# Experts' loop: transposes, combine, gather and the S5 operators in pieces between weight tiles, and six more weight buffers

## The chip, the cores and the metric

The kernel runs on one core of one Trainium2 chip. The metric is the device time of one execution in microseconds (us). One launch computes the whole model.

## What is computed

All in float32, for 512 tokens of 1024 channels: a first block (a convolution branch and a recurrent branch, then a mixture of experts), and a second block (attention and a gated feed-forward layer, then a state space layer, S5, and again a feed-forward layer). The change lies in the mixture of experts, in which each of 16 experts picks its 64 best tokens:

```python
def expert_choice_moe(h, p):
    cap = EC_CAPACITY * T // N_EXPERTS                      # 2 * 512 / 16 = 64
    affinity = jax.nn.softmax(h @ p['router_w'], axis=-1)
    gates, idx = lax.top_k(jnp.swapaxes(affinity, 1, 2), cap)
    xe = jax.vmap(lambda hb, ib: hb[ib])(h, idx)
    hid = jax.nn.silu(einsum('becd,edf->becf', xe, p['exp_w1'])) * einsum('becd,edf->becf', xe, p['exp_w3'])
    ye = einsum('becf,efd->becd', hid, p['exp_w2']) * gates[..., None]
    return jax.vmap(lambda ib, yb: zeros((T, D)).at[ib.reshape(-1)].add(yb.reshape(-1, D)))(idx, ye)
```

Each expert's w1 and w3 are 1024 x 2048, its w2 is 2048 x 1024: 16 experts have 402.65 MB of weights, which are read once. S5's operators (the taps of a convolution inside chunks of 8 tokens, and the map from a chunk to the state) depend on that layer's parameters alone; the kernel computes them early, beside the experts, and keeps them in DRAM.

## The kernel before

Experts are taken in eight pairs, j = 0 to 7 (`moe`, L1512). A pair reads 48 weight tiles of 128 x 2048 (1 MiB), in order: 16 of w1 and w3 for each of the two experts, then 16 of w2. SP issues each load (`pair_weight`, L1331) as soon as its buffer is free. Pairs 1 to 7 have the stream's six buffers (`open_stream`, L1225); pair 0 has fifteen, nine of them in memory that is given back afterwards (`open_early`).

Inside a pair, for each expert e and each of four groups fb of four w13 tiles: PE multiplies the 64 gathered tokens (XG) with the four tiles, the products for w1 above those for w3 (L1537); ACT copies the result out of PSUM (hs, L1543); PE transposes it in four parts (L1546); ACT takes the tanh (L1549) and DVE makes silu times the other product from it (L1550, L1551), which gives hid. After both experts come the w2 tiles, two at a time (L1580). At the pair's end ACT copies the result (ye, L1604), DVE makes the scaled one-hot matrix Gt (L1607), and eight matmuls (L1613) with one PSUM buffer spread ye over the tokens; after each of them DVE adds it to acc (L1619; in pair 0 it copies, L1617).

The next pair's tokens are gathered after the first expert (`gather`, L1477): PE selects the indices (L1484), DVE compares (oh, L1488), 32 products with the one-hot matrix follow (L1505, each recorded as two), and ACT writes XG (L1509).

`s5_prep` (L1969) begins at the end of pair 0: a set-up on DVE, then eight pieces q. For each, an engine (POOL for q = 1, 4, 6, DVE for the others) makes complex products, big (also called CA) and Winc, by `cmul` (L1957, L1958: pairs of products and their sum); PE transposes Winc in two halves (L2058), ACT copies them (sst, L2060) and stores them (s5i, L2061); the same engine makes a block-diagonal factor bbd (L2064, L2068); PE multiplies big by it (L2072) and ACT and DVE finish a slice of KT (L2075, L2076). big and Winc have a name for each engine (bigv, Wincv, bigg, Wincg) and one buffer for each name. In the source, one step of this stands behind each group of four tiles.

The order of the source isn't the order on the engines: the framework's scheduler orders each engine's instructions, and each engine then works through its own list. The rows of the list are shown below where they matter.

```python
        pool, n = self.early[x % len(self.early)] if self.early else (None, 0)
        w = self.wslot("we") if pool is None else pool.tile([P, 2048], F32, name="we", tag="we", bufs=n)
        self.nc.sync.dma_start(w, src)
```

## Time and profile before

| | us |
|---|---|
| median of 3 runs | 3466.82 |
| lowest and highest | 3463.49, 3468.05 |
| span of the profiled execution | 3452.7 |
| PE busy in it | 3168.8 (92%) |
| DVE busy in it | 1735.9 (50%) |
| ACT busy in it | 963.4 (28%) |
| POOL busy in it | 672.3 (19%) |

The span is that of one execution from its first to its last instruction; the profiled execution's own time isn't given, and the median of the runs lies 14.1 us above the span. The experts' first load is issued at 895.7 us in the span; their pairs begin at 983 (pair 0), 1110.6, 1298.4, 1424.3, 1549.8, 1677, 1804 and 1930 (pair 7), and end at 2056. The rows read are in a section below. In them PE is the matmul, PEld the load of its stationary operand, and an arrow in square brackets names what an engine had waited for.

### The profile page before, as it was taken

What the parts mean: (1) busy time and instruction counts of PE and PEld (TensorE: products, weight loads), DVE (VectorE), ACT (ScalarE), POOL (GpSimd) and SP (SyncE); (2) the same over time, 40 slices, a digit from 0 to 9 for tenths busy, and PEclk for the clock granted to TensorE, in tenths of its full rate; (3) what the DMA queues carried; (4) which work ended last, traced back from release to release, by engine and by line L of the source; (5) the groups of instructions that cost most, each with busy time, mean ns of one, the idle gap of its engine ahead of it and who ended that gap; (6) DMA issues with size and microseconds to landing.
All of it is one profiled execution on the core that took longest, in us unless ns stands there. A gap on an engine that the chain in (4) does not pass through costs nothing.

```text
span 3452.7 us, 41189 instructions
## 1 busy us (share of the span) xinstructions
PE 3168.8 (92%) x15981; PEld 1954.8 (57%) x15981; DVE 1735.9 (50%) x3105; ACT 963.4 (28%) x1799; POOL 672.3 (19%) x703
## 2 busy tenths in 40 slices
PE   8988999999999689999999989799888998999999
PEld 3746566666563333233333227565767877778887
DVE  4656777664451831101101117887477775556464
ACT  3303444443121111111001013227332332234242
POOL 1032234332110520000000003310397002110000
PEclk9989989898899899999999999899999999999999
DMA  5743211112568589999999984320335555522221
GB/s 213 249 163 97 68 47 47 44 35 99 218 240 338 214 341 395 411 410 386 402 406 389 396 339 159 134 87 18 112 117 207 177 200 139 154 87 94 95 98 67
DMA packets 145481, 681.33 MB, mean 197 GB/s; under 512 B 25455, under 2 KB 34839, under 8 KB 77320
## 3 DMA queue, kind: packets, MB, share of 16 engines
q1 hardware_dynamic: 135520, 652.99, 50.0%
q0 software_dynamic: 5392, 17.64, 1.4%
q10 hardware_dynamic: 4376, 8.09, 0.7%
q8 instruction: 126, 2.06, 0.2%
q14 instruction: 67, 0.55, 0.0%
HBM read 654.54 MB, written 24.12 MB: 197 GB/s over the span
## 4 chain that ended last, share of the span: by engine, by line
PE 51%; DMA 8%; POOL 7%; DVE 6%; ACT 2%; issue 2%; SPq 0%; ACTq 0%; POOLq 0%; DVEq 0%
PE mm L1537 12%; DMA we<-in_w_dram 7%; PE mm L284 5%; PE mm L285 5%; PE mm L286 5%; PE ch L1580 3%; POOL cug L1957 3%; PE tr L1505 2%; PE sm L1613 2%; POOL sca L1958 2%; PE sm L286 1%; PE sm L285 1%; PE sm L284 1%; PE tr L1546 1%; PE ch L284 1%
## 5 line engine op out<-in xcount | busy, mean ns | idle before, releaser
L1537 PE MATMUL mm<-we,XG 128*64 128x512 f32 x2048 | 495.3, 608 | 4.8 <-DMA we<-in_w_dram 4.1
L1537 PEld LDWEIGHTS mm<-we,XG 128*64 128x64 f32 x2048 | 139.3, 138 | 292.2 <-issue 269.0
L1580 PE MATMUL ch<-we,hid 128*64 128x512 f32 x1024 | 278.2, 601 | 26.3 <-DMA we<-in_w_dram 26.3
L284 PE MATMUL mm<-hh,wh 128*128 128x512 f32 x704 | 282.7, 402 | 20.7 <-DVE vg L1911 16.4
L285 PE MATMUL mm<-hl,wh 128*128 128x512 f32 x704 | 278.7, 396 | 0.0
L286 PE MATMUL mm<-hh,wl 128*128 128x512 f32 x704 | 272.9, 396 | 0.0
L1550 DVE SCALAR_TENSOR_TENSOR hth<-hth,tr 128x256 f32<-128x256 f32 x64 | 26.9, 420 | 446.2 <-ACT hth L1549 446.1
L1580 PEld LDWEIGHTS ch<-we,hid 128*64 128x64 f32 x1024 | 95.4, 136 | 201.7 <-issue 139.1
L1619 DVE TENSOR_TENSOR acc<-acc,sm 128x512 f32<-128x512 f32 x48 | 33.0, 687 | 292.1 <-PE sm L1613 292.1
L284 PEld LDWEIGHTS mm<-hh,wh 128*128 128x128 f32 x704 | 134.7, 191 | 63.5 <-issue 27.0
L1543 ACT ACTIVATE hs<-mm 128x512 f32<-128x512 f32 x64 | 38.2, 597 | 465.7 <-PE mm L1537 448.8
L1626 POOL TENSOR_TENSOR ess<-ess,mhalf 128x1 f32<-128x1 f32 x4 | 2.6, 650 | 811.3 <-DVE ess L1625 811.2
L346 DVE SCALAR_TENSOR_TENSOR macc<-wa,cvs,macc 128x512 f32<-128x512 f32 (+1 forms) x119 | 152.8, 1300 | 12.9 <-DMA wa<-in_adaw_dram 10.4
L279 DVE TENSOR_TENSOR wl<-wu,wh 128x1024 fp32r<-128x1024 f32 x88 | 115.4, 1312 | 80.5 <-ACT wh L278 80.2
L286 PEld LDWEIGHTS mm<-hh,wl 128*128 128x128 f32 x704 | 134.8, 191 | 29.6
L285 PEld LDWEIGHTS mm<-hl,wh 128*128 128x128 f32 x704 | 135.3, 192 | 26.7 <-POOL hl L455 0.3
L461 POOL TENSOR_TENSOR X<-X,gy 128x512 f32<-128x512 f32 x20 | 28.2, 1434 | 587.6 <-DVE gy L1643 587.6
L278 ACT ACTIVATE wh<-wu 128x1024 fp32r<-128x1024 f32 x88 | 93.2, 1060 | 131.5 <-PE mm L285 98.6
L279 DVE TENSOR_TENSOR wl<-wd,wh 128x1024 fp32r<-128x1024 f32 (+1 forms) x48 | 56.0, 1168 | 95.3 <-ACT wh L278 91.0
L284 PE MATMUL mm<-hTh,wh 128*128 128x512 f32 x208 | 88.3, 425 | 6.1 <-ACT th L795 5.5
L278 ACT ACTIVATE wh<-wd 128x1024 fp32r<-128x1024 f32 (+1 forms) x48 | 47.5, 989 | 164.0 <-PE sm L286 79.6
L286 PE MATMUL mm<-hTh,wl 128*128 128x512 f32 x208 | 88.3, 424 | 3.5 <-DVE wl L279 3.5
(841 smaller groups left out, 6753.9 us busy)
## 6 DMA issues: line engine op xcount, KB each, us to landing
we<-in_w_dram SPq DMA_DIRECT2D x384, 1024.0 KB, 9.5
wu<-in_wupf_dram SPq DMA_DIRECT2D x44, 1024.0 KB, 4.8
wa<-in_adaw_dram SPq DMA_DIRECT2D x24, 1024.0 KB, 5.1
wa<-in_adaw_dram SPq DMA_DIRECT2D x96, 256.0 KB, 4.1
wa<-in_modw_dram SPq DMA_DIRECT2D x16, 1024.0 KB, 5.7
wd<-in_wdn_dram SPq DMA_DIRECT2D x16, 1024.0 KB, 4.8
aw<-in_awin_dram SPq DMA_DIRECT2D x12, 1024.0 KB, 5.0
wi<-in_win_dram SPq DMA_DIRECT2D x46, 256.0 KB, 2.7
```

Source lines behind the costliest of these rows:

```text
L278: self.nc.scalar.activation(h, x, AF.Copy)
L279: (E or self.nc.vector).tensor_tensor(l, x, h.bitcast(F32), op=OP.subtract)
L284: mm(ps, a[0], b[0], start=start, stop=False)
L285: mm(ps, a[0], b[1], start=False, stop=False)
L286: mm(ps, a[1], b[0], start=False, stop=stop)
L346: V.scalar_tensor_tensor(a, w, c, a, op0=OP.mult, op1=OP.add)
L1505: nc.tensor.matmul(ps[:, c * i:c * i + c], self.xn[:, t, o:o + P], oh[:, t], start=(t == 0), stop=(t == TT - 1), skip_group_check=True)
L1537: nc.tensor.matmul(ps[64 * h:64 * h + 64], XG[:, k, CAP * e:CAP * e + CAP], w[:, i, h], start=(k == 0), stop=(k == KD - 1), skip_group_che ...
L1580: nc.tensor.matmul(py[n][64 * h:64 * h + 64], hid[h][:, f], ww[h][:, i, 512 * n:512 * n + 512], start=(f == 0), stop=(f == 15), skip_group ...
L1613: nc.tensor.matmul(pc, G[:, P * t:P * t + P], ye[:, 512 * n:512 * n + 512], start=not last, stop=True, skip_group_check=last)
L1957: E.tensor_tensor(u[k], p[k][1], p[k][0], op=OP.mult)
L1958: E.tensor_tensor(o, u[0], u[1], op=op)
```

## The change

1. The transposes, tanh and gate products of a group of four tiles (`gated`) are issued behind the first tile of the next group.
2. The gather of the next pair is a generator that is stepped behind the first tile of each group of the second expert, so that its selection, and two halves of the channels, come apart.
3. The combine of a pair is a generator too, stepped in the next pair: one matmul and one addition behind each of the second to fourth tiles of a group. Only the last pair does it at once, and its sums of the experts before (`moe_sum`) stand inside the w2 tiles.
4. `s5_prep` makes the vector products of a piece (`vectors`, now with bbd) a step ahead of its matmuls (`products`); even pieces go to DVE, odd ones to POOL; bbd has a buffer for each engine; it is stepped twelve times in a pair, and what is left of it is done when pair 3 begins. s5k is stored from POOL's queue.
5. From pair 3 on, when the memory of `s5_prep` is given back, every second weight tile goes into a pool of six more buffers (`late`).

Comments are removed as well, which is left out here.

```diff
     def pair_weight(self, j, x):
...
-        src = self.I["w13"][2 * j + x // 16, x % 16] if x < 32 else self.I["w2"][j, x - 32]
...
         pool, n = self.early[x % len(self.early)] if self.early else (None, 0)
         w = self.wslot("we") if pool is None else pool.tile([P, 2048], F32, name="we", tag="we", bufs=n)
-        self.nc.sync.dma_start(w, src)
+        self.nc.sync.dma_start(w, self.weight_src(j, x))
...
+    def weight_src(self, j, x):
+        return self.I["w13"][2 * j + x // 16, x % 16] if x < 32 else self.I["w2"][j, x - 32]
...
     def gather(self, j, wk):
...
             for t in range(TT):
                 nc.vector.tensor_scalar(oh[:, t], po[:, :P], self.m("tcol")[:, t:t + 1], None, op0=OP.is_equal)
+            yield
             parts = [(oh, XG)]
...
     def moe(self):
...
+        NJ = NEXP // 2
...
                 g0 = self.gather(0, wk)
                 nxt = next(g0)
-                prep = ()
+                prep, late, acc, MG = (), None, None, None
+                turn = cycle(range(2))
                 def weight(x):
-                    return self.first_w[x] if j == 0 and x < len(self.first_w) else self.pair_weight(j, x)
-                for j in range(NEXP // 2):
+                    if j == 0:
+                        return self.first_w[x] if x < len(self.first_w) else self.pair_weight(j, x)
+                    if late is None or next(turn):
+                        return self.pair_weight(j, x)
+                    w = late.tile([P, 2048], F32, name="we", tag="we", bufs=6)
+                    nc.sync.dma_start(w, self.weight_src(j, x))
+                    return w
+                def gated(hs, hT, fb):
+                    pt = self.psum("tr", 2)
+                    for i in range(4):
+                        nc.tensor.transpose(pt[:, P * i:P * i + P], hs[:, P * i:P * i + P], self.ident)
+                    pv = pt.rearrange("p (i h s) -> p i h s", i=4, h=2)
+                    th = wk.tile([P, 4, CAP], F32, name="hth")
...
+                def combine(j, G, ye):
...
+                        for n in range(2):
+                            pc = self.psum("sm", 1)
+                            nc.tensor.matmul(pc, G[:, P * t:P * t + P], ye[:, 512 * n:512 * n + 512], start=True, stop=True)
+                            s = slice(512 * n, 512 * n + 512)
+                            if j == 0:
+                                nc.vector.tensor_copy(acc[:, t, s], pc)
+                            else:
+                                nc.vector.tensor_tensor(acc[:, t, s], acc[:, t, s], pc, op=OP.add)
+                            yield
+                def run():
+                    nonlocal pend
+                    if pend is not None:
+                        gated(*pend)
...
+                pend, comb, gat = None, iter(()), iter(())
+                for j in range(NJ):
                     XG = nxt
+                    last = j == NJ - 1
+                    if j == 3:
+                        for _ in prep:
+                            pass
+                        s5s.close()
+                        late = self.pool(es, "late", side="right")
                     hid = []
                     for e in range(2):
                         hT = wk.tile([P, 16, CAP], F32, name="hid", bufs=3)
                         hid.append(hT)
+                        if e and not last:
+                            gat = self.gather(j + 1, wk)
                         for fb in range(4):
                             ps = self.psum("mm", 2)
                             for kq in range(4):
                                     for h in range(2):
                                         nc.tensor.matmul(ps[64 * h:64 * h + 64], XG[:, k, CAP * e:CAP * e + CAP], w[:, i, h],
                                                          start=(k == 0), stop=(k == KD - 1), skip_group_check=True)
-                            if j:
-                                for _ in islice(prep, 1):
-                                    pass
+                                if kq == 0:
+                                    run()
+                                    if e:
+                                        nxt = next(gat, None) or nxt
+                                else:
+                                    next(comb, None)
+                                if j and (kq == 0 or kq == 2 and fb % 2):
+                                    next(prep, None)
                             hs = wk.tile([P, 512], F32, name="hs")
                             nc.scalar.activation(hs, ps, AF.Copy)
-                            pt = self.psum("tr", 2)
...
+                            pend = hs, hT, fb
...
-                        if e == 0 and j < NEXP // 2 - 1:
-                            nxt, *_ = self.gather(j + 1, wk)
-                    last = j == NEXP // 2 - 1
...
-                        sums = {}
-                        for i, tag in enumerate(("mm", "mm", "tr", "tr", "sm", "pp")):
-                            sums[i // 2, i % 2] = self.moe_sum(tag, acc, i // 2, i % 2)
                     py = [self.psum("ch", 2) for _ in range(2)]
                     for q in range(8):
                         ww = []
...
-                    if last:
-                        for _ in prep:
-                            pass
+                        if q == 0:
+                            run()
+                            for _ in gat:
+                                pass
+                        if q == 2 and last:
+                            sums = {}
+                            for i, tag in enumerate(("mm", "mm", "tr", "tr", "sm", "pp")):
+                                sums[i // 2, i % 2] = self.moe_sum(tag, acc, i // 2, i % 2)
...
-                            prep = self.s5_prep(self.pool(es, "s5p", side="right"))
+                            prep = self.s5_prep(self.pool(s5s, "s5p", side="right"))
+                            next(prep)
...
                         G = wk.tile([P, T], F32, name="Gt", bufs=1)
                         nc.vector.tensor_scalar(G, self.m("iota"), self.gcol[:, 0, j:j + 1], self.gcol[:, 1, j:j + 1],
                                                 op0=OP.is_equal, op1=OP.mult)
-                    ss = wk.tile([P, TT, 2], F32, name="ess", bufs=1)
-                    for t in range(TT):
...
-                            nc.tensor.matmul(pc, G[:, P * t:P * t + P], ye[:, 512 * n:512 * n + 512], start=not last, stop=True,
-                                             skip_group_check=last)
-                            s = slice(512 * n, 512 * n + 512)
-                            if j == 0:
-                                nc.vector.tensor_copy(acc[:, t, s], pc)
-                            elif not last:
-                                nc.vector.tensor_tensor(acc[:, t, s], acc[:, t, s], pc, op=OP.add)
-                            else:
-                                sums[t, n] = pc
...
+                    if not last:
+                        comb = combine(j, G, ye)
+                ss = wk.tile([P, TT, 2], F32, name="ess", bufs=1)
+                for t in range(TT):
...
...
-        for q in range(KD):
-            E = G if q in (1, 4, 6) else V
-            t = "v" if E is V else "g"
+        def vectors(q):
...
+            E, t = ((V, "v"), (G, "g"))[q % 2]
             s = slice(NQ * q, NQ * q + NQ)
             CA = wk.tile([P, 1152], F32, name="big" + t).rearrange("p (r i c j) -> p r i c j", r=2, i=NQ, c=16)
...
-            yield
             self.cmul(E, wk, *[W[:, r].rearrange("p i c j -> p i j c") for r in range(2)],
...
+            bd = wk.tile([P, 2, NQ, 2, 16], F32, name="bbd" + t)
+            E.memset(bd, 0.0)
+            for g in range(2):
+                rs = slice(64 * g, 64 * g + 64)
+                for r in range(2):
+                    E.tensor_scalar(bd[rs, r, :, g], bb[rs, r, s], 1.0 - 2 * r, None, op0=OP.mult)
+            return CA, W, bd
+        def products(q, CA, W, bd):
             for r in range(2):
                 ps = self.psum("pp", 1)
                 for i in range(NQ):
...
                 st = wk.tile([P, 512], F32, name="sst", bufs=2)
                 nc.scalar.activation(st, ps, AF.Copy)
                 nc.scalar.dma_start(self.s5i[q, :, r], st.rearrange("p (i c) -> p i c", c=P))
-            yield
-            bd = wk.tile([P, 2, NQ, 2, 16], F32, name="bbd")
-            E.memset(bd, 0.0)
-            for g in range(2):
-                rs = slice(64 * g, 64 * g + 64)
-                for r in range(2):
-                    E.tensor_scalar(bd[rs, r, :, g], bb[rs, r, s], 1.0 - 2 * r, None, op0=OP.mult)
+                yield
...
-        nc.sync.dma_start(self.s5k[:, :, 112:].rearrange("q p x -> p q x"), KT.rearrange("p q j c -> p q (j c)"))
+        yield
+        ops = None
+        for q in range(KD + 1):
+            new = vectors(q) if q < KD else None
+            yield
+            if ops is not None:
+                yield from products(q - 1, *ops)
+            ops = new
+        nc.gpsimd.dma_start(self.s5k[:, :, 112:].rearrange("q p x -> p q x"), KT.rearrange("p q j c -> p q (j c)"))
```

Where this puts the instructions is seen in the lists of the engines.

PE in the first group of pair 4 (sm: the combine of pair 3; mm: the product with w1 and w3; tr: the transposes; misc is the identity). Before, from the sixth combine product on:

```order
L1537 MATMUL mm<-we,XG 64x512 x2
L1613 MATMUL sm<-ye,Gt 128x512
L1537 MATMUL mm<-we,XG 64x512 x2
L1613 MATMUL sm<-ye,Gt 128x512
L1537 MATMUL mm<-we,XG 64x512 x4
L1546 MATMUL tr<-misc,hs 128x128 x4
L1537 MATMUL mm<-we,XG 64x512 x3
```

and with the change, from the fourth on:

```order
L1552 MATMUL sm<-ye,Gt 128x512
L1588 MATMUL mm<-we,XG 64x512 x4
L1552 MATMUL sm<-ye,Gt 128x512
L1540 MATMUL tr<-misc,hs 128x128 x4
L1588 MATMUL mm<-we,XG 64x512 x4
L1552 MATMUL sm<-ye,Gt 128x512
L1588 MATMUL mm<-we,XG 64x512 x4
```

Before, all eight combine products stood in the group's four tiles, with two matmuls (half a tile) between them; now a whole tile (four matmuls here) lies between two of them, the fifth stands ahead of the group's transposes, and the last three in the next group.

PE in pair 1, around the gather (tr with oh: the gather; pp: S5's transposes and products). Before:

```order
L2072 MATMUL pp_8462<-bigv_8346,bbd_8456 32x128 x8
L1537 MATMUL mm_8190<-we_8203,XG_7528 64x512 x4
L1537 MATMUL mm_8190<-we_8209,XG_7528 64x512 x4
L2058 MATMUL pp_8531<-misc_65,Wincv_8474 128x128 x4
L1546 MATMUL tr_8243<-misc_65,hs_8241 128x128 x4
L1505 MATMUL tr_8261<-oh_8256,xn2_6574 128x128 x16
L1505 MATMUL tr_8282<-oh_8256,xn2_6574 128x128 x16
L1537 MATMUL mm_8304<-we_8305,XG_7528 64x512 x4
```

and with the change, where the last S5 piece and the gather meet:

```order
L2118 MATMUL pp_9354<-bigg_9037,bbdg_9059 32x128
L1588 MATMUL mm_8314<-we_8397,XG_7536 64x512 x4
L2118 MATMUL pp_9354<-bigg_9037,bbdg_9059 32x128 x7
L1540 MATMUL tr_8412<-misc_65,hs_8403 128x128 x4
L1508 MATMUL tr_8421<-oh_8333,xn2_6574 128x128
L1588 MATMUL mm_8405<-we_8406,XG_7536 64x512 x4
L1508 MATMUL tr_8421<-oh_8333,xn2_6574 128x128 x15
L1588 MATMUL mm_8405<-we_8450,XG_7536 64x512 x4
L1588 MATMUL mm_8405<-we_8456,XG_7536 64x512 x4
L1588 MATMUL mm_8405<-we_8462,XG_7536 64x512 x4
L1540 MATMUL tr_8477<-misc_65,hs_8468 128x128 x4
L1508 MATMUL tr_8486<-oh_8333,xn2_6574 128x128 x2
```

The gather stood as one block of 32 in front of the second half of S5's products; now its first half stands behind all of them, with one product ahead of a weight tile and fifteen behind it, and its second half comes in the next group. All of S5's products are still in pair 1. The transposes (tr_8477) stand directly behind their group's last tile, ahead of the next group's first; so they do in all pairs but pair 0, where a whole tile was put ahead of them.

POOL in pair 1, the second of its S5 pieces. Before:

```order
L1957 TENSOR_TENSOR cug_8731<-scc,pw 128x576
L1957 TENSOR_TENSOR cug_8733<-scc,pw 128x576
L2064 MEMSET bbd 128x256
L2068 TENSOR_SCALAR bbd<-bb 64x4x16 x4
L1958 TENSOR_TENSOR bigg<-cug_8731,cug_8733 128x4x9x16
L1957 TENSOR_TENSOR cug_8736<-scc,pw 128x576
L1957 TENSOR_TENSOR cug_8738<-scc,pw 128x576
L1958 TENSOR_TENSOR bigg<-cug_8736,cug_8738 128x4x9x16
L1957 TENSOR_TENSOR cug_8777<-bb,pw 128x512
L1957 TENSOR_TENSOR cug_8779<-bb,pw 128x512
L1958 TENSOR_TENSOR Wincg<-cug_8777,cug_8779 128x4x8x16
L1957 TENSOR_TENSOR cug_8782<-bb,pw 128x512
```

and with the change:

```order
L2000 TENSOR_TENSOR cug_8351<-scc,pw 128x576
L2000 TENSOR_TENSOR cug_8353<-scc,pw 128x576
L2001 TENSOR_TENSOR bigg<-cug_8351,cug_8353 128x4x9x16
L2099 MEMSET bbdg 128x256
L2000 TENSOR_TENSOR cug_8356<-scc,pw 128x576
L2000 TENSOR_TENSOR cug_8358<-scc,pw 128x576
L2103 TENSOR_SCALAR bbdg<-bb 64x4x16 x2
L2001 TENSOR_TENSOR bigg<-cug_8356,cug_8358 128x4x9x16
L2103 TENSOR_SCALAR bbdg<-bb 64x4x16 x2
L2000 TENSOR_TENSOR cug_8361<-bb,pw 128x512
L2000 TENSOR_TENSOR cug_8363<-bb,pw 128x512
L2001 TENSOR_TENSOR Wincg<-cug_8361,cug_8363 128x4x8x16
```

The factor bbd stood ahead of the piece's first result, between two pieces; now it stands inside the piece, ahead of Wincg.

## Rows read from the trace of the kernel before

**Rows 1.** Page, section 2: the span in 40 slices of 86.3 us.

```profile
DMA  5743211112568589999999984320335555522221
GB/s 213 249 163 97 68 47 47 44 35 99 218 240 338 214 341 395 411 410 386 402 406 389 396 339 159 134 87 18 112 117 207 177 200 139 154 87 94 95 98 67
```

**Rows 2.** Busy time in stretches: PE, PEld, DVE, ACT, POOL, then PEclk, DMA share, GB/s.

```profile
983.00:1110.60 127.60, 123.03 (x635) 58.12 (x635) 32.19 (x112) 20.95 (x49) 3.33 (x6) 0.96 0.79 314
1110.60:1298.40 187.80, 147.86 (x693) 57.98 (x692) 108.22 (x197) 25.55 (x53) 72.83 (x57) 0.90 0.74 280
1549.80:1677.00 127.20, 116.53 (x501) 43.02 (x500) 13.81 (x29) 12.09 (x27) 0.00 (x0) 1.00 0.98 398
1480.00:1540.00 60.00, 54.53 (x225) 18.64 (x222) 3.36 (x8) 3.92 (x8) 0.00 (x0) 1.00 1.01 418
1560.00:1580.00 20.00, 18.50 (x77) 6.00 (x76) 5.48 (x13) 1.96 (x4) 0.00 (x0) 1.00 0.93 337
1140.00:1160.00 20.00, 5.78 (x20) 2.29 (x22) 19.99 (x19) 1.20 (x2) 17.00 (x11) 0.64 0.37 133
```

**Rows 3.** Timeline of PE: start, duration, what, and the idle time before it.

```profile
1358.76 7.08 PE L1537 MATMUL mm<-we,XG 128*64 128x512 f32 x30
1366.59 0.66 PE L1546 MATMUL tr<-misc,hs 128*128 128x128 f32 x4 [0.75 <-ACT hs L1543]
...
1552.11 1.13 PE L1613 MATMUL sm<-ye,Gt 128*128 128x512 f32 x2
...
1758.37 1.94 PE L1537 MATMUL mm<-we,XG 128*64 128x512 f32 x8 [0.26 <-DMA we<-in_w_dram]
1760.86 1.94 PE L1537 MATMUL mm<-we,XG 128*64 128x512 f32 x8 [0.55 <-DMA we<-in_w_dram]
```

**Rows 4.** Chain of waits: pair 1's and pair 7's last weight tiles have landed.

```profile
1294.85 3.65 PE ch L1580 x12
...
2051.97 3.65 PE ch L1580 x12
```

**Rows 5.** Groups by line, PE, pair 3 (1424.3 to 1549.8 us).

```profile
L1505 PE MATMUL tr<-oh,xn 128*128 128x128 f32 x64 | 7.3, 275 | 0.0
L1546 PE MATMUL tr<-misc,hs 128*128 128x128 f32 x32 | 5.2, 286 | 4.6 <-ACT hs L1543 4.6
L1484 PE MATMUL sm<-gf,misc 16*128 16x64 f32 x4 | 0.7, 282 | 0.0
```

**Rows 6.** Waits of PE in pair 0 (983 to 1110.6): total, times, longest.

```profile
PE tr L1546 <- ACT hs L1543: 3.7, 5, 0.7
```

**Rows 7.** Waits of PE in pair 1 (1110.6 to 1298.4 us).

```profile
PE pp L2058 <- DVE Wincv L1958: 25.4, 3, 12.7
```

**Rows 8.** Timeline of PE in pair 1.

```profile
1166.66 0.66 PE L2058 MATMUL pp<-misc,Wincg 128*128 128x128 f32 x4
...
1170.50 1.12 PE L2072 MATMUL pp<-bigg,bbd 128*32 128x128 f32 x14
...
1259.71 1.11 PE L2072 MATMUL pp<-bigv,bbd 128*32 128x128 f32 x12
```

**Rows 9.** Timeline of POOL in pair 1.

```profile
1102.51 0.63 POOL L1980 DMA_DIRECT2D sa<-in_s_a_dram  x1 [88.83 <-PE ch L1580]
...
1134.38 2.94 POOL L1957 TENSOR_TENSOR cug<-scc,pw 128x576 f32<-128x576 f32 x2
...
1164.20 3.61 POOL L2068 TENSOR_SCALAR bbd<-bb 64x64 f32<-64x64 f32 x4
1171.82 2.42 POOL L1958 TENSOR_TENSOR bigg<-cug,cug 128x576 f32<-128x576 f32 x1 [4.02 <-PE pp L2072]
...
1186.97 1.97 POOL L1958 TENSOR_TENSOR Wincg<-cug,cug 128x512 f32<-128x512 f32 x1
```

**Rows 10.** Timeline of DVE in pair 1.

```profile
1134.56 3.38 DVE L1957 TENSOR_TENSOR cuv<-scc,pw 128x576 f32<-128x576 f32 x2
...
1165.00 1.47 DVE L1957 TENSOR_TENSOR cuv<-scc,pw 128x576 f32<-128x576 f32 x2
```

41 lines of the change are left out of this document (20 added, 21 removed).

## The prediction

> **What bounds the kernel now.** I start with the page's slices. From slice 16 to slice 23 the DMA line reads 9 and the bandwidth 386 to 411 GB/s, which nothing else in the program reaches [rows 1]. These are the pairs of experts 2 to 7. The stretches then say how close that is to a limit. One pair takes 127.2 us at 398 GB/s with PE busy 116.53; sixty microseconds inside pair 3 run at 418 GB/s and a DMA share of 1.01; twenty just behind a pair's boundary run at 337 [rows 2]. So the transfers are the limit in most of a pair, and they pause near its boundary. The timeline of PE shows what the limit is: where PE waits for a weight tile, one starts at 1758.37 and the next at 1760.86, 2.49 us apart [rows 3]. 48 tiles make 119.5 us, about 7 less than a pair takes.
>
> The transfers stop because PE falls behind and holds the buffers. I read that from three rows. Eight combine products stand at the boundary, 1.13 us each (1.05 to the next start), between pieces of the first tiles [rows 3]; the gather of the next pair is one block of 64 matmuls, 7.3 us, in mid pair [rows 5]; and each of a pair's eight groups of four tiles ends with transposes before which PE waits 0.75 us for ACT's copy of the product [rows 3], 4.6 us in a pair where it was counted [rows 5]. A load can only be issued once a buffer is released. The group of four tiles with the eight combine products takes PE 7.08 + 0.66 + 0.75 + 9.0 = 17.5 us, 7.5 more than four loads; the one with the gather takes 15.8, 5.8 more. Together that is 13.3 us of lag, of which 7 are lost, so six buffers forgive some 3 us at a time; I use that figure below.
>
> Pair 1 is another matter. It takes 187.8 us at 280 GB/s [rows 2], because PE stands behind the S5 operators: 25.4 us of its idle time go to DVE's Wincv in three waits [rows 7], and from 1140 to 1160 PE is busy for 5.78 us and the granted clock falls to 0.64 [rows 2]. Pair 0 is bound by PE (123.03 busy of 127.6, DMA share 0.79) [rows 2].
>
> **Pairs 2 to 7.** The change takes the blocks apart. The order has one combine product per weight tile over the first two groups, and the gather in two halves of 16 operands, in the last two groups of the first products. The transposes, a tile late in the source, stand directly behind their group's last tile in the order of these pairs, so their wait of 0.75 us stays; only in the first two groups does a combine product or the selection stand ahead and cover it. PE's own work stays: eight groups at 7.08 + 0.66, [rows 3] eight pairs of w2 tiles at 3.65 [rows 4], 7.3 for the gather and 0.7 for its selection [rows 5], eight combine products at 1.13 and six waits at 0.75 [rows 3]. That is 61.9 + 29.2 + 8.0 + 9.0 + 4.5 = 112.6 us, 7 below the 119.5 of the loads. The worst group of four tiles is now 7.08 + 0.66 + four combine products of 1.13, 12.3 us, or with half a gather and the wait 12.1, against 10.0 for four loads. PE falls behind by 2.3 us in each of a pair's first two groups and 2.1 in each of the two with the gather, and catches up 1.5 in each of the four between and 10 in the w2 tiles. The most it collects is 4.6 us, against 3 that six buffers forgive: pair 2 may lose 1.5, and with twelve buffers, from pair 3 on, nothing is lost. I let the loads run without a pause but for that. From the last tile of pair 1, landed at 1294.85, to that of pair 7 at 2051.97 lie 757.1 us [rows 4]; 288 tiles at 2.49 take 717.1, and 1.5 for pair 2. **Term: −38.5 us.** If each pair kept 1.5 (the buffers no help) it would be −31; if none did, −40. So the six extra buffers carry at most 7 of it, and most comes from the blocks taken apart. Their first load must wait until the S5 memory is free, but the products of S5 end at 1261 [rows 8], over 150 us before pair 3, so that wait costs nothing.
>
> **Pair 0.** Here the order does have a whole tile ahead of the transposes, so the five waits for ACT, 3.7 us in all [rows 6], go; the loads have room there. **Term: −4 us.** The deferral of the combine out of the pair's end only moves it into pair 1. S5's set-up starts when the last w2 products release POOL's loads [rows 9], so it comes 4 us sooner as well.
>
> **Pair 1.** The source spreads the S5 pieces over pairs 1 to 3, but the order shows that all products stay in pair 1, now ahead of the gather instead of around it. What changes is who computes: POOL gets four pieces (1, 3, 5, 7) instead of three, DVE four instead of five. A POOL piece is serial with PE: its first result may be written when the products of the piece before have read that buffer. Before, the wait ended at 1171.82 and the last Wincg at 1188.94, 17.1 us [rows 9]; the block-diagonal factor bbd, 3.6 us, stood in the shadow of PE's turn and now stands inside the piece; PE's turn from the second transposes to the last product was 1166.66 to 1171.62, 4.9 us [rows 8]. The period is 17.1 + 3.6 + 4.9 = 25.6 us. PE is through with the first POOL piece at 1171.6 as before [rows 8], with the other three at 1197.2, 1222.8 and 1248.4, less the 4 us of pair 0: 1244.4, against 1260.8 now [rows 8]. Behind it now stand eight tiles at 1.77, the gather and two transposes, 14.2 + 7.3 + 1.3 = 22.8 us, where one tile stood, so PE comes to the w2 tiles near 1267, some 5 us later than now. Eight tiles in 22.8 us leave the loads 8 × 2.49 = 19.9, so they gain about 3 of that. **Term for pairs 0 and 1 together, pair 0's 4 us inside: +2 us.** Bounds: bbd wholly in the shadow again, three times 3.6, gives −9; each period 4 us longer, about what DVE's pair of products loses twice beside POOL [rows 10], gives +14. I take +2, with the row of the piece that had DVE beside it. The clock, 0.64 in the worst stretch, stays as long as PE waits there.
>
> The SP queue loses one transfer (s5k) to POOL's and is passed by nothing else; behind the last pair the order is nearly unchanged, and I cost it at nothing since PE's chain there is the same.
>
> **Sum:** −38.5 + 2 = −36.5 us. The profiled span is 3452.7, so the changed one would be 3416; the median is 3466.8, and the 14.1 that lie around the span stay. 3466.8 − 36.5 = **3430 us**.
>
> **Rivals.**
> *POOL becomes the bound of pair 1 and eats the gain* (the slower side). The four pieces are serial, and the combine's DVE additions and DVE's own pieces run beside them. For it speaks that DVE's pair of 576-element products took 3.38 us beside POOL and 1.47 alone [rows 10]. Three periods count, so break-even is at 25.6 + 36.5 / 3 = 37.8 us each; at 42 the time would be 3430 + 49 = 3479. Against it: the one period that is seen has DVE at work inside its 17.1. Chance 0.03.
>
> *DVE and POOL exclude each other.* By the rows a POOL piece takes 17.1 with DVE in part beside it, and DVE's pair of products loses 1.9 us beside POOL [rows 9, 10]. If they excluded each other wholly, a DVE piece, four pairs of products at 1.47 and their four sums, about 9 us, would be added to POOL's work, less what the 17.1 already hold and PE's turn hides: I estimate 2 to 3 us a period, 6 to 9 in all, 3438. Chance 0.12. The Trainium skill ("SBUF — State Buffer", "Who interferes with whom") states that a DVE instruction with two SBUF inputs and a GpSimd instruction that reads SBUF hold a shared port in turn, the loser fully blocked; the rows agree with a loss and leave open whether it is whole.
>
> *S5 is shorter than I make it* (POOL's pieces as fast as without DVE beside them, and PE's turn in the shadow): pair 1 ends 11 us sooner, 3419. Chance 0.12.
>
> *The S5 work does spread over pairs 1 to 3*, as the source reads: pair 1 would come down from 187.8 to about 130, and the time to some 3372. The order speaks against it. Chance 0.03.
>
> *The loads don't keep 2.49 us without a pause*, or PE's slips still stop them: the gain of pairs 2 to 7 is then a third or less, 3456 and up. Sixty microseconds at 418 GB/s speak against it [rows 2]. Chance 0.05. The Trainium skill ("DMA: Bandwidth & Descriptors", "Specifications") puts the limit of HBM for one core at some 358 GB/s, by which no pair could be under 140 us; the trace has 127.2 and decides.
>
> **How the numbers follow.** My forecast, the loads' pace in pairs 2 to 7 and pair 1 within its bounds, has 0.65. The range 3408 to 3446 takes in most of its bounds (−40 − 9 gives 3418 and −31 + 14 gives 3450, both ends at once being unlikely), the second and the third rival, and 10 us below for slips of PE in pairs 0 and 1 that I have not counted; it leaves out the first, fourth and fifth, 0.11. A measurement of this kernel can tell about 0.2%, 7 us, from no change: faster by more than that are the forecast, rivals two to four and part of the fifth, 0.94; the same 0.03; slower 0.03.
>
> **What would show it.** Right: from pair 2 on, 119 to 120 us from boundary to boundary, a DMA share near 1.0 in every 20 us, and PE waiting for weight tiles in every group; the transposes' wait for ACT's copy gone in pair 0 and left six times in a later pair; pair 3, where the six buffers come, no more than 2 us shorter than pair 2; pair 1 still near 185 us, with PE waiting for POOL's Wincg, and the last S5 product near 1244. Wrong: stretches of 340 GB/s that remain at boundaries; a first extra load that waits; S5 products beyond 1260; or PE busy near 119 in a pair, which would mean that the loads no longer set the pace.

## The result, and the profile after

The changed kernel takes **3420.72 us** (median of 4 runs, 3415.78 to 3428.51) against 3466.39 for the kernel before, run beside it (4 runs, 3463.49 to 3468.05): ratio 0.9874, 95% interval 0.9854 to 0.9893, or 45.7 us less (37 to 51). The forecast was 3430, the range 3408 to 3446. The profiled execution spans 3416.5 us.

The page's slices, to hold against [rows 1]:

```profile
DMA  5643211111659689999999965310336465422221
GB/s 216 240 162 113 66 44 47 44 38 65 246 217 380 242 307 414 419 421 421 421 421 421 421 259 187 111 68 1 120 130 205 164 216 139 152 81 96 96 99 68
```

From slice 16 to 23 the transfers run at 414 to 421 GB/s; before, they went between 386 and 411. The same stretches as in [rows 2] (pair 0, pair 1, pair 2, pair 3, and 20 us in pair 1's S5 part):

```profile
984.20:1101.60 117.40, 117.14 (x618) 54.14 (x618) 26.74 (x84) 19.66 (x47) 3.02 (x6) 0.99 0.86 341
1102.30:1289.80 187.50, 147.32 (x693) 55.92 (x693) 99.81 (x180) 25.26 (x53) 89.83 (x74) 0.91 0.76 287
1289.80:1410.70 120.90, 112.86 (x502) 43.03 (x502) 13.82 (x29) 12.05 (x27) 0.00 (x0) 1.00 1.01 415
1410.70:1531.10 120.40, 112.60 (x501) 42.87 (x501) 13.82 (x29) 12.04 (x26) 0.00 (x0) 1.00 1.01 421
1130.00:1150.00 20.00, 17.16 (x72) 5.91 (x72) 19.90 (x21) 3.05 (x6) 17.96 (x11) 0.82 0.38 135
```

A later pair takes 119.8 to 120.8 us; before, they took 125.5 to 127.2. Pair 1 is as long as it was. The chain of waits, pair 1's and pair 7's last tiles ([rows 4]):

```profile
1286.22 3.65 PE ch L1620 x12
...
2007.77 3.65 PE ch L1620 x12
```

721.55 us lie between them, 2.505 for each of 288 tiles, where there were 757.1. What SP, which issues the loads, waited for from 1430 to 1550 us: in the kernel before, in the changed one (L1533 loads into the six more buffers), and in e1_six below, the changed kernel without those (total, times, longest):

```profile
SPq L1331 <- PE mm L1537: 67.7, 32, 10.0
SPq L1331 <- PE ch L1580: 34.4, 15, 5.3
```

```profile
SPq L1533 <- DMA we<-in_w_dram: 51.2, 24, 2.9
SPq L1330 <- DMA we<-in_w_dram: 50.5, 24, 2.3
```

```profile
SPq L1330 <- PE mm L1587: 70.0, 32, 4.8
```

Before, a load waited for PE to give back a buffer, once for 10 us. In the changed kernel it waits for transfers ahead of it, 2 to 3 us each. That it no longer waits for PE is the work of the six more buffers; e1_six has nearly all of the gain of pairs 2 to 7 with loads that wait for PE as before, but never longer than 4.9 us.

The profiled executions by stage, from the first w13 product and from the end of each pair's last w2 product, all in us; the rows below the first two belong to the experiments:

| kernel | experts start | pair 0 | pair 1 | pairs 2–7 | after pair 7 | span | median, ratio to before |
|---|---|---|---|---|---|---|---|
| before | 987.5 | 123.2 | 187.8 | 757.1 | 1397.1 | 3452.7 | 3466.39 |
| changed | 984.2 | 117.4 | 188.3 | 721.5 | 1405.1 | 3416.5 | 3420.72, 0.9874 [0.9854, 0.9893] |
| c_after | 993.9 | 118.3 | 188.8 | 720.2 | 1407.2 | 3428.4 | 3422.65, 0.9882 [0.9861, 0.9902] |
| e1_six | 996.7 | 118.2 | 194.6 | 725.6 | 1409.2 | 3444.3 | 3440.57, 0.9916 [0.9884, 0.9949] |
| e2_late_only | 995.1 | 123.4 | 185.9 | 728.6 | 1409.5 | 3442.5 | 3443.03, 0.9919 [0.9887, 0.9951] |
| e3_combine_end_six | 1001.6 | 118.1 | 195.5 | 747.4 | 1407.6 | 3470.2 | 3453.91, 0.9972 [0.9956, 0.9988] |
| e13_gather_block_six | 995.6 | 119.4 | 182.9 | 740.2 | 1401.7 | 3439.8 | 3440.62, 0.9934 [0.9906, 0.9962] |
| e4_s5_before | 992.0 | 117.5 | 179.2 | 724.1 | 1405.4 | 3418.2 | 3421.75, 0.9881 [0.9853, 0.9908] |
| e8_gated_at_once | 985.7 | 122.8 | 187.3 | 722.7 | 1399.8 | 3418.3 | 3424.08, 0.9893 [0.9869, 0.9917] |
| e7_s5_dve | 996.5 | 121.8 | 158.9 | 722.8 | 1403.8 | 3403.8 | 3397.43, 0.9802 [0.9769, 0.9834] |
| e11_before_dve | 1004.3 | 123.1 | 167.8 | 755.2 | 1401.5 | 3451.9 | 3448.73, 0.9951 [0.9931, 0.9971] |
| e5_spread | 994.9 | 117.9 | 131.8 | 781.0 | 1403.1 | 3428.7 | 3429.59, 0.9894 [0.9870, 0.9918] |
| e9_s5_w2 | 996.1 | 118.3 | 124.3 | 787.8 | 1401.2 | 3427.7 | 3426.75, 0.9885 [0.9863, 0.9908] |
| e12_s5_w2_two | 989.2 | 118.2 | 126.1 | 741.7 | 1397.1 | 3372.3 | 3385.57, 0.9761 [0.9737, 0.9785] |

Within the experts the change gives 5.8 + 35.6 − 0.5 = 40.9 us. The rest of the difference of the two spans, 36.2, is 3.3 less ahead of the experts and 8.0 more behind them, where the same code runs. Over the profiles of the table the first of those two stages moves by 20 us and the second by 12 (last section); so the experiments below are read mostly from the pairs' lengths, which came out alike in the two profiles of the changed kernel (720.2 and 721.5).

### The profile page after: what moved, and what is told of

Its sections match the earlier page's. It is cut to its first block, busy times and chain, and to the rows that moved or that the text cites. A ratio compares the mean times of both kernels' runs of the same rounds, so it can differ in the third digit from the quotient of the medians.

```text
span 3416.5 us, 41161 instructions
## 1 busy us (share of the span) xinstructions
PE 3156.0 (92%) x15981; PEld 1962.0 (57%) x15981; DVE 1727.5 (51%) x3088; ACT 961.3 (28%) x1799; POOL 688.6 (20%) x721
## 4 chain that ended last, share of the span: by engine, by line
PE 39%; DMA 19%; POOL 7%; DVE 7%; issue 2%; ACT 2%; SPq 0%; POOLq 0%; ACTq 0%; DVEq 0%
DMA we<-in_w_dram 18%; PE mm L1588 5%; PE mm L284 5%; PE mm L285 5%; PE mm L286 5%; POOL cug L2000 3%; PE ch L1620 2%; POOL sca L2001 2%; PE sm L286 1%; PE sm L285 1%; PE sm L284 1%; PE tr L1508 1%; DMA wa<-in_adaw_dram 1%; PE ch L284 1%; PE ch L286 1%
## 5 line engine op out<-in xcount | busy, mean ns | idle before, releaser
L1588 PE MATMUL mm<-we,XG 128*64 128x512 f32 x2048 | 482.6, 609 | 4.6 <-DMA we<-in_w_dram 3.7
L1620 PE MATMUL ch<-we,hid 128*64 128x512 f32 x1024 | 267.0, 600 | 16.8 <-DMA we<-in_w_dram 16.7
L1620 PEld LDWEIGHTS ch<-we,hid 128*64 128x64 f32 x1024 | 96.4, 136 | 180.2 <-issue 131.8
L279 DVE TENSOR_TENSOR wl<-wu,wh 128x1024 fp32r<-128x1024 f32 x88 | 115.4, 1313 | 75.2 <-ACT wh L278 74.9
L461 POOL TENSOR_TENSOR X<-X,gy 128x512 f32<-128x512 f32 x20 | 28.2, 1430 | 589.3 <-DVE gy L1686 589.2
```

The lines of the kernel that those rows point to most:

```text
L279: (E or self.nc.vector).tensor_tensor(l, x, h.bitcast(F32), op=OP.subtract)
L1588: nc.tensor.matmul(ps[64 * h:64 * h + 64], XG[:, k, CAP * e:CAP * e + CAP], w[:, i, h], start=(k == 0), stop=(k == KD - 1), skip_group_che ...
L1620: nc.tensor.matmul(py[n][64 * h:64 * h + 64], hid[h][:, f], ww[h][:, i, 512 * n:512 * n + 512], start=(f == 0), stop=(f == 15), skip_group ...
```

## Experiments

Theory: the blocks in PE's work (eight combine products at a boundary, the gather in mid pair) made PE hold the buffers; taken apart, they fit into what six buffers forgive, and the six more carry little. Rivals: the extra buffers do it; or the S5 split does.

**Again, the changed kernel (c_after).** No edit; run beside e5_spread, e7_s5_dve and e8_gated_at_once.

> The changed kernel once more, as the reference of the three that follow. Every theory: 3421 us within 6; pair 0 at 117.4, pair 1 at 188, pairs 2 to 7 at 119.8 to 120.8 us each.

Measured: 3422.65 us (6 runs). The pairs repeat within 1.0 us, the start of the experts moves by 9.7.

**The pieces alone (e1_six).** The six late buffers are left out.

```diff
-                        late = self.pool(es, "late", side="right")
```

> The change without the six extra buffers. Theory 'pieces' (taking the combine and the gather apart is what lets the loads run): nothing is lost, 3421 us within 6, and each of the pairs 2 to 7 stays at 118 to 120.5 us, the first two included. Theory 'buffers' (the extra buffers do it from pair 3 on): pairs 3 to 7 go back to 125 to 127 us, so 3450 to 3456.

Pairs 2 to 7 take 725.6 us, 4.1 more than with twelve buffers and 31.5 less than before. For these pairs the pieces suffice. The median is 20 us above the changed kernel's, where the expectation had at most 6; by the profiles pairs 1 to 7 account for 10 us, and the rest lies ahead of the experts and behind them, where the code is the same. Pair 1's 6 us more are no effect of the buffers, which come in pair 3: its instruction lists differ a little, and PE has a wait of 5.0 us for ACT's hs there that the changed kernel doesn't have.

**The buffers alone (e2_late_only).** The kernel before, blocks and all, with every second tile from pair 3 on in six late buffers.

```diff
+                    if late is None or next(turn):
+                        return self.pair_weight(j, x)
+                    w = late.tile([P, 2048], F32, name="we", tag="we", bufs=6)
...
+                    if j == 3:
...
+                        late = self.pool(es, "late", side="right")
```

> The kernel before with nothing but the six extra buffers from pair 3 on; the combine and the gather stay blocks. Theory 'pieces or buffers, either is enough' (a block puts PE 7.5 us behind, twelve buffers forgive that): pair 2 stays at 126, pairs 3 to 7 come to 119 to 121, 3466 - 30 = 3436 us within 6. Theory 'pieces alone': the blocks still stop the loads, pairs at 124 to 127, 3460 to 3468.

Pair 2 keeps its 125.8 us, pair 3 takes 122.5, pairs 4 to 7 take 120.1 on average. So twelve buffers cover both blocks whole. In these pairs pieces and buffers are substitutes: each gives nearly all of the gain from where it starts, together they give 4.1 us over the pieces. The median, 3443.03, is just above what was expected.

**One block issued whole: the combine (e3_combine_end_six), then the gather (e13_gather_block_six),** both without the late buffers.

```diff
-                        comb = combine(j, G, ye)
+                        for _ in combine(j, G, ye):
+                            pass
```

> The change without the extra buffers and with the combine whole at the pair's end again; the gather stays in pieces. If the combine's block is the larger cause, as its lag of 7.5 us against the 5.8 of the gather has it, and six buffers forgive 3 us: pairs 2 to 7 at 123 to 124.5, 3421 + 25 = 3446 us within 8. If the two blocks only hurt together, or the gather was the cause: pairs at 120 or less, 3421 to 3426.

```diff
-                        if e and not last:
-                            gat = self.gather(j + 1, wk)
...
+                        if e == 0 and not last:
+                            nxt, *_ = self.gather(j + 1, wk)
```

> The changed kernel without its six late buffers, with the gather issued whole after the first expert as before and the combine still in pieces (e3_combine_end_six is the other half: combine whole, gather in pieces). From the last tile of pair 1 to that of pair 7 it took 757.1 us with both blocks, 747.4 with the combine's alone, 725.6 with neither. Theory A (a block costs what PE falls behind in its group less some 3 us that six buffers forgive; the gather's group is 15.8 us against 10.0 for its loads, so 2.8 us a pair): 725.6 + 6 x 2.8 = 742. Theory B (the two blocks' losses add, so the gather's is what the combine's left over, 757.1 - 747.4 = 9.7): 735. Theory C (the combine's block was the whole cause; the gather's block alone is forgiven): 724 to 728.

With the combine whole, pairs 2 to 7 take 747.4 us, 21.8 over e1_six or 3.6 a pair; with the gather issued whole 740.2, 14.6 over or 2.9 in each of the five pairs that gather (pair 7, with no pair behind it, takes 120.7). The prediction had PE lag by 7.5 us in the one group and 5.8 in the other: six buffers forgive 3.9 and 2.9 of it, which is Theory A, with the "some 3 us" as its only fitted number. The two losses together (36.4) exceed the 31.5 that both blocks cost in the kernel before, so they don't simply add.

The gather is issued whole in e13, but it is no block on PE. In the kernel before, its 64 matmuls ran without a break (7.31 us from 1468.43); here the scheduler put whole tiles between them:

```profile
1455.04 0.61 PE L1508 MATMUL tr<-oh,xn 128*128 128x128 f32 x4
1455.58 1.94 PE L1585 MATMUL mm<-we,XG 128*64 128x512 f32 x8
1457.45 1.60 PE L1508 MATMUL tr<-oh,xn 128*128 128x128 f32 x12
...
1467.65 2.94 PE L1508 MATMUL tr<-oh,xn 128*128 128x128 f32 x24
```

All of it still falls into five tiles, and the pair loses all the same. So to stop the loads the work needn't stand in one piece; it is enough that one group of tiles has to carry it, and it has to be spread over several groups.

**The S5 split undone (e4_s5_before):** the former s5_prep, five pieces on DVE and three on POOL, one step after each group of four tiles.

```diff
-        def vectors(q):
...
-            E, t = ((V, "v"), (G, "g"))[q % 2]
+        for q in range(KD):
+            E = G if q in (1, 4, 6) else V
...
```

> The change with the S5 operators made as before (five pieces on DVE, three on POOL, the pieces stepped once in a group). Theory 'S5's part gives nothing' (pair 1 took 187.8 us before and 187.5 after): 3421 us within 6, pair 1 at 185 to 190. Rival 'S5's part gives some of the gain, which the combine beside it takes back': pair 1 at 195 or more, 3430 and up.

Pair 1 takes 179.2 us, 9.1 less than in the changed kernel; the medians can't be told apart. So no gain of the S5 part can be seen. That it cost its own pair 9 us isn't shown: with the S5 part unchanged, pair 1 lies between 182.9 and 195.5 in e13, e1 and e3, as the scheduler orders it.

**The transposes at once (e8_gated_at_once).**

```diff
-                            pend = hs, hT, fb
+                            gated(hs, hT, fb)
```

> The change with the transposes and gate products issued at once, right behind the group's last tile in the source. The order of pairs 2 to 7 is the same for them, only pair 0's changes. Theory 'the deferral gives pair 0's waits for ACT and nothing else': pair 0 from 117.4 to 121 to 123, pairs 2 to 7 at 119.8 to 120.8, 3425 us within 6. Rival 'it is what frees the loads': pairs 2 to 7 at 123 or more, 3440 and up.

Pair 0 goes back to 122.8 us (117.4), pairs 2 to 7 together stay. The deferral is worth 5.4 us, in pair 0 alone, where the scheduler had left it in place. Only 1.5 of it are waits for ACT; most of the rest is in the w13 products, which keep PE busy for 63.1 us there and for 59.7 in the changed kernel. (In e7_s5_dve pair 0 takes 121.8 us with the deferral and without a wait for ACT: the granted clock was 0.50, its lower level, in the first 10 us of it, against 0.85 in the changed kernel.)

**Every S5 piece on DVE (e7_s5_dve, and e11_before_dve in the kernel before),** big and Winc with two buffers, in e7 bbd too.

```diff
-            E, t = ((V, "v"), (G, "g"))[q % 2]
+            E, t = V, "v"
...
-            CA = wk.tile([P, 1152], F32, name="big" + t).rearrange("p (r i c j) -> p r i c j", r=2, i=NQ, c=16)
+            CA = wk.tile([P, 1152], F32, name="big" + t, bufs=2).rearrange("p (r i c j) -> p r i c j", r=2, i=NQ, c=16)
...
```

> The change with all eight S5 pieces on DVE, in two buffers of each of big, Winc and bbd; POOL is left out of the pieces. Theory 'DVE and POOL take time from each other': a DVE piece alone is about 11 us, eight make 88 and PE's turns lie beside them, so the last S5 product comes 10 to 20 us sooner after the set-up than with two engines and pair 1 is 175 to 182 us, 3409 to 3416. Rival 'they run beside each other with little loss': eight pieces on one engine take longer than four on each of two, pair 1 at 200 or more, 3433 and up.

> The kernel before with all eight S5 pieces on DVE, in two buffers, and nothing else changed. Theory 'DVE and POOL hold each other up': pair 1 falls from 187.8 to 158 to 170 us, 3466 - 24 = 3442 us within 10, without anything of the change. Rival 'it helped only together with the change's stepping': pair 1 at 183 or more, 3460 to 3468.

Pair 1 takes 158.9 us instead of 188.3, less than the theory had, and the median falls to 3397.43. In the kernel before, nearly the same edit takes 20 us off pair 1 with nothing of the change. The groups by line show one cause. DVE in the changed kernel, POOL at work beside it (1120 to 1230 us; busy time, mean ns of one):

```profile
L2000 DVE TENSOR_TENSOR cuv<-scc,pw 128x576 f32<-128x576 f32 x16 | 18.4, 1177 | 0.0
L2103 DVE TENSOR_SCALAR bbdv<-bb 64x64 f32<-64x64 f32 x16 | 9.7, 637 | 0.1
```

DVE in e7_s5_dve, with POOL idle (1130 to 1260 us):

```profile
L2000 DVE TENSOR_TENSOR cuv<-scc,pw 128x576 f32<-128x576 f32 x32 | 22.8, 754 | 0.2
L2103 DVE TENSOR_SCALAR bbdv<-bb 64x64 f32<-64x64 f32 x32 | 5.1, 197 | 0.2
```

POOL in the changed kernel (1120 to 1230 us), and in e9_s5_w2 below, where DVE makes no S5 piece:

```profile
L2000 POOL TENSOR_TENSOR cug<-scc,pw 128x576 f32<-128x576 f32 x16 | 25.0, 1582 | 0.4
```

```profile
L1999 POOL TENSOR_TENSOR cug<-scc,pw 128x576 f32<-128x576 f32 x32 | 38.3, 1216 | 0.7
```

The same product takes DVE 754 ns alone and 1177 beside POOL, POOL 1216 and 1582; DVE's small bbd factors take 197 and 637. The trace of the changed kernel has both cases within 5 us. POOL waited for PE until 1155.15 (its rows stand in the next section); two products of DVE took 1.29 us in that pause and 3.28 just behind it:

```profile
1152.99 1.29 DVE L2000 TENSOR_TENSOR cuv<-bb,pw 128x512 f32<-128x512 f32 x2
...
1155.78 3.28 DVE L2000 TENSOR_TENSOR cuv<-bb,pw 128x512 f32<-128x512 f32 x2
```

So the two engines hold each other up: that is the mechanism of the second rival. It depends on what they do: two products of DVE took 1.47 us [rows 10] while POOL was at its bbd factors (1164.20 to 1167.81 in [rows 9]), as fast as alone. The Trainium skill ("SBUF — State Buffer", "Who interferes with whom") has a DVE instruction with two SBUF inputs and a GpSimd instruction that reads SBUF take turns at a shared port; these rows agree that both lose. Whether one is shut out wholly, they leave open: at the prices alone, S5's products, sums and factors of the changed kernel would take DVE 44.3 us and POOL 64.5, 108.8 one after the other, and both were through in 101 (1120.7 to 1221.8), but POOL's times are rough.

How much of the 29 us is this isn't shown, as the edit also gives the tiles two buffers. In the changed kernel, with one buffer for each engine's, POOL waited 12.9 us and DVE 3.5 for PE to have read the piece before; in e7 DVE never did. Two engines with two buffers each were not run.

**S5 spread for good over pairs 1 to 7 (e5_spread).** One step in each of a pair's middle groups; so that the scheduler keeps it there, big's first element and the PSUM tile of the transposes are first written from that group's hid. No late buffers.

```diff
-                                if j and (kq == 0 or kq == 2 and fb % 2):
+                                if j and kq == 0 and (fb > 1 and e == 0 or fb < 2 and e == 1):
                                     next(prep, None)
...
+            E.tensor_copy(CA[:, 0:1], self.mark)
...
+                if r == 0:
+                    V.tensor_copy(ps[:, 0:1], self.mark)
```

> The change with its S5 work really spread over pairs 1 to 7: a one-column copy of hid into big and into the PSUM tile of the first transposes ties each piece to the group of tiles behind which the source steps it (four steps in a pair, in the middle groups); no extra buffers, since the S5 memory stays in use. Theory 'pair 1 is long only because all S5 work sits in it, and PE has room for about one piece in each pair': pair 1 comes from 188 to 120 to 124 us, the others to at most 122, so 3421 - 60 = 3361 us within 12. Rival 'PE's room is used up (112.6 of 119.5 us), a piece's 3 us and its waits are paid in full in each pair': pairs 1 to 7 at 124 to 128, 3390 to 3415.

Pair 1 falls by 57 us and pairs 2 to 7 give all of it back: 781.0 against 721.5 (and 725.6 in e1_six, which has no late buffers either). The median, outside what either theory gave, can't be told from the changed kernel's. PE waits for ACT's hs 40.9 us in pairs 1 to 7, once for 8.5, where it waits 31.0 in the changed kernel, and in three waits 6.4 us for the writes that tie the piece down. That is less than was lost; the rest stays open.

**S5 between w2 tiles of pairs 1 to 6, all on POOL (e9_s5_w2, one buffer; e12_s5_w2_two, two).** The same ties, from the w2 tile's own data; no late buffers.

```diff
+                        if j and q in (1, 2, 4, 5, 6):
+                            self.mark = ww[0][:, 0, 0:1]
+                            next(prep, None)
```

> The change with S5's matmul steps put one by one between the w2 tiles of pairs 1 to 6 (five steps in a pair, each tied by a one-column copy of the weight tile that lands there) and all pieces on POOL; no extra buffers. Theory 'S5 cost 66 us only because its pieces came as blocks where PE had no room; the w2 tiles leave PE 10 us a pair': pairs 1 to 6 at 120 to 122 us each, 3421 - 62 = 3359 us within 10. Rival 'a piece costs some 9 us wherever it stands, as in the run that spread the pieces over the middle groups': pairs 1 to 6 at 128 to 135, 3420 to 3435. With DVE out of the pieces, POOL's product of 576 elements should take less than the 1.58 us that it took beside DVE's pieces if the two engines hold each other up, the same if POOL is simply slower.

> The kernel of e9_s5_w2 (the S5 steps between w2 tiles of pairs 1 to 6, every product on POOL, no late buffers) with two buffers each for bigg, Wincg and bbdg instead of one. Theory (e9's pairs of 124 to 141 us were long because POOL, with one bigg buffer, waited for PE's reads of the one before, and its tie copy held a weight buffer all that time; PE's longest wait for Wincg was 7.3 us): with two of each the longest wait of PE's pp matmuls for Wincg falls below 2 us, the weight loads' wait for bbdg goes, pairs 1 to 6 run at 120 to 124 us, pair 1 some 64 us shorter than the change's 188, the median some 3360 us (3350 to 3380). Rival (a piece costs PE's room wherever it stands, about 9 us by e5_spread): pairs 2 to 6 stay at 126 to 136, the median 3405 to 3430, about that of e9_s5_w2 (3427).

With one buffer pair 1 takes 124.3 us, but pairs 2 to 6 between 128 and 141. Its median is where the rival had it. Two waits stand out, PE's for Wincg and SP's for a weight buffer that POOL still had to read (pairs 1 to 7; total, times, longest):

```profile
PE pp L2112 <- POOL Wincg L2000: 29.7, 5, 7.3
```

```profile
SPq L1330 <- POOL bbdg L2100: 13.7, 7, 2.5
```

With two buffers, the only difference, PE waits for Wincg no more, SP waits for POOL once (4.8 us), and pairs 1 to 6 take 122.9 to 126.1 us. Pairs 1 and 2 of it:

```profile
1107.40:1233.50 126.10, 116.30 (x525) 43.87 (x525) 29.29 (x112) 15.57 (x34) 47.59 (x54) 1.00 0.98 393
1233.50:1358.20 124.70, 117.00 (x533) 43.94 (x534) 14.78 (x35) 14.73 (x32) 24.08 (x25) 1.00 1.01 412
```

The first theory of that expectation holds in kind; its sum was too good by 25 us. S5 adds some 4 us to PE's busy time in a pair (117.00 against 112.60), and pairs 2 to 7 are 16 us longer than in e1_six; that the one makes the other is argued, not shown. At **3385.57 us** (ratio 0.9761, 0.9737 to 0.9785) it is the fastest kernel here, 35 us below the change and 80 below the kernel before.

## Why the prediction came out

**Pairs 2 to 7: right in kind and size, −35.6 us against −38.5.** The pace is 2.505 us a tile, not 2.49, which is 4.3 us over 288 tiles; against it, of the 1.5 us taken for pair 2 at most 0.5 was lost (120.8 here, 120.4 in c_after). The extra buffers carry 4.1 us where "at most 7" was said. PE's groups came as worked out: the group with four combine products takes 11.7 us from 1410.59 to 1422.28 and 0.6 for its transposes, as said 12.3; the one with half a gather from 1470.19 to 1482.54, 12.35 us against 12.1.

```profile
1470.19 0.65 PE L1540 MATMUL tr<-misc,hs 128*128 128x128 f32 x4 [0.76 <-ACT hs L1599]
1470.68 0.61 PE L1508 MATMUL tr<-oh,xn 128*128 128x128 f32 x4
1471.22 1.94 PE L1588 MATMUL mm<-we,XG 128*64 128x512 f32 x8
1473.09 3.39 PE L1508 MATMUL tr<-oh,xn 128*128 128x128 f32 x28
1476.41 5.37 PE L1588 MATMUL mm<-we,XG 128*64 128x512 f32 x24
1482.54 0.66 PE L1540 MATMUL tr<-misc,hs 128*128 128x128 f32 x4 [0.76 <-ACT hs L1599]
```

The signs named for it came too: a DMA share of 1.01 or 1.02 in every 20 us from 1410 to 1550, pair 3 only 0.4 us shorter than pair 2, seven waits for ACT left in a pair where six were said.

**A row misread without harm: "eight pairs of w2 tiles at 3.65 [rows 4]".** That row counts 12 products; a pair of tiles has 16. The size came out right even so: in pair 0, where the w2 products wait for no tile, four pairs of tiles take 13.95 us, 3.49 each, and all eight with what stands between them keep PE busy for 30.1, where the prediction had 29.2.

```profile
1079.70 13.95 PE L1620 MATMUL ch<-we,hid 128*64 128x512 f32 x64
```

In pair 3 the same products count as 33.3 us, at the same granted clock of 1.00:

```profile
1512.49 4.42 PE L1620 MATMUL ch<-we,hid 128*64 128x512 f32 x16 [0.53 <-DMA we<-in_w_dram]
```

```profile
L1588 PE MATMUL mm<-we,XG 128*64 128x512 f32 x256 | 58.9, 599 | 0.8 <-DMA we<-in_w_dram 0.8
L1620 PE MATMUL ch<-we,hid 128*64 128x512 f32 x128 | 33.3, 601 | 2.3 <-DMA we<-in_w_dram 2.3
L1540 PE MATMUL tr<-misc,hs 128*128 128x128 f32 x32 | 5.2, 285 | 4.7 <-ACT hs L1599 4.7
```

There the two tiles of a pair land one after the other. In the trace's single records one of the two series of products goes on alone from 1514.26, until at 1514.98 the other comes out of a wait. So part of the wait for tiles is recorded as busy time, and PE's 112.6 us in pair 3 are more than its work. With pair 0's 27.9 to 30.1 for the w2 products and the 4.7 of waits for ACT, PE needs 112 to 114 us, which is the prediction's 112.6. One sign didn't come: PE is seen waiting for weight tiles in six places in a pair, 3.1 us in all, and not "in every group".

**Pair 0: −5.8 us against −4.** ACT's wait is gone from it, and e8_gated_at_once shows that the deferral is the cause. The prediction counted the five waits alone, 3.7 us; the w13 products, busy for 59.7 us where they were for 61.5, make most of the rest.

**Pair 1: +0.5 us against +6 (the +2 for both pairs, less pair 0's −4); the first step of three held, two missed.** What PE waited for (total, times, longest):

```profile
PE pp L2110 <- POOL Wincg L2001: 17.9, 4, 8.4
PE sm L1552 <- DVE acc L1555: 7.4, 1, 7.4
PE pp L2110 <- DVE Wincv L2001: 4.3, 3, 2.8
```

PE's wait moved from DVE's Wincv [rows 7] to POOL's Wincg, as predicted. The period held: POOL's first result of each later piece waits for PE's reading of the one before,

```profile
1155.15 1.74 POOL L2001 TENSOR_TENSOR bigg<-cug,cug 128x576 f32<-128x576 f32 x1 [6.72 <-PE pp L2118]
...
1181.71 1.43 POOL L2001 TENSOR_TENSOR bigg<-cug,cug 128x576 f32<-128x576 f32 x1 [3.72 <-PE pp L2118]
...
1207.07 1.42 POOL L2001 TENSOR_TENSOR bigg<-cug,cug 128x576 f32<-128x576 f32 x1 [2.47 <-PE pp L2118]
```

26.6 and 25.4 us apart, against 25.6. That is also why the second rival, whose mechanism is real, added nothing: the row the period was made from had DVE at work in it. (The 1.47 us that the prediction calls "alone" were taken beside POOL's factors, as said above; the price is that of e7 all the same, 754 ns for one.)

*First miss: "PE is through with the first POOL piece at 1171.6 as before".* The last S5 product ends at 1227.2, not 1244.4, and the first piece is where it comes from:

```profile
1153.84 1.13 PE L2118 MATMUL pp<-bigg,bbdg 128*32 128x128 f32 x14
...
1226.09 1.13 PE L2118 MATMUL pp<-bigg,bbdg 128*32 128x128 f32 x14
...
1252.38 4.13 PE L1620 MATMUL ch<-we,hid 128*64 128x512 f32 x18
```

It is done at 1154.97, 12.6 us ahead of the 1167.6 that the prediction used (1171.6 less 4). Of that, 3.3 are the experts' earlier start in this execution and 1.8 pair 0's larger gain; 7.5 are the step's. Before, PE came to it only after a DVE piece for which it had waited until 1158.55; with the vector products a step ahead, that piece was ready. The last period is shorter too, 20.3 us from the end of one piece's products to the next, as DVE has no piece left beside it. That makes the other 5 us.

*Second miss: the loads that follow.* PE comes to the w2 tiles at 1252.38. Counted from the pair's start that is 9.6 us sooner than the prediction's 1267, but the pair is only 5.5 us shorter than predicted. The prediction had the loads gain on PE before the w2 tiles, which would leave 33.4 us for these (1267 to 1300.4); they took 37.4, and 34.4 before. The likely reason, not tried by itself: while PE waited in the S5 part, the buffers were held and few loads went out, 135 GB/s from 1130 to 1150 us, so the last tiles are still to be loaded when PE comes early. A part of its earliness is lost there, but not all of it: in e4_s5_before PE comes to the w2 tiles 143.7 us into the pair, against 150.8, and the pair is 9.1 us shorter.

*Not foreseen:* the combine of pair 0, now in pair 1, frees its PSUM buffer by a DVE copy that stands behind S5 in DVE's queue, and PE waits 7.4 us for it. The prediction costed that move at nothing without naming the work that hides it. What that wait costs the pair was not tried by itself.

**The sum.** The terms gave −36.5 and the stages show −40.9, inside the bounds of the terms; pairs 2 to 7 gave 2.9 us less than forecast, pair 0 1.8 more and pair 1 5.5 more, so the errors cancel in part. The forecast of 3430 was 9 us too high: 4 from the terms, and 5 that lie inside the interval of the gain (37 to 51 us). The 14.1 us between span and median before were no fixed work around the span, as the prediction had it: every timed run on record lies 1.7 to 2.3 us above its span, so the rest was that one execution's distance from the median.

## What to carry to other kernels

In a loop paced by loads, compare the other work that each group of tiles has to carry with what the buffers forgive. Spread that work over more groups or add buffers: here either removed the stall, and both together added little. Read from the engine's own list where the scheduler put a piece. Moving the same S5 work out of pair 1 cost pairs 2 to 7 between 16 and 62 us over e1_six, by where its pieces stood and how many buffers they had. Before splitting work over two engines, time the operation alone and beside the other.

## What the runs showed of the hardware that had not been expected

The code ahead of the experts is the same in all these kernels, and yet they start between 984.2 and 1004.3 us. The granted clock goes with it, if not strictly: over the first 960 us it is 0.92 where they start earliest and 0.89 in the two profiles where they start latest. The stretch from 400 to 600 us in the changed kernel, then in e11_before_dve:

```profile
400.00:600.00 200.00, 187.57 (x1352) 125.44 (x1352) 147.82 (x323) 88.13 (x198) 74.95 (x65) 0.91 0.15 48
```

```profile
400.00:600.00 200.00, 187.12 (x1313) 124.58 (x1312) 141.72 (x311) 87.23 (x195) 69.50 (x62) 0.87 0.15 49
```

PE is as busy in both, 187 of 200 us, and gets fewer instructions done (1313 against 1352) at the lower mean between the clock's two levels, 1.2 and 2.4 GHz. What decides the grant wasn't found. A change of 10 us in the experts can't be read from one span of this kernel; it can from the pairs.

The transfers kept 419 to 421 GB/s for 600 us on this core alone. The Trainium skill ("DMA: Bandwidth & Descriptors", "Specifications") gives some 358 GB/s as HBM's limit for a core, a stack's 716 divided by two cores; this kernel on its one core was not held to it. The fifth rival, loads that don't keep their pace, falls by the same rows.
